# Layer 0's feed-forward for latent and context tokens in one set of gate and up products, with w2 accumulated in PSUM

## The chip, the cores and the metric

One core of a Trainium2 chip runs the whole program. The metric is the device time of one execution in microseconds, the median over runs. TensorE (PE) does the matmuls, VectorE (DVE), ScalarE (ACT) and GpSimd (POOL) the elementwise work, SyncE (SP) issues the DMAs; PE writes its sums to PSUM, eight banks of 512 float32 columns on 128 partitions, everything else lies in SBUF.

## The reference

Two transformer layers over 512 latent tokens and 256 context tokens of width 1024. What the change touches is layer 0's feed-forward (hidden width 2816), which both token kinds pass with the same weights and different modulation:

```python
def swiglu(h, w13, w2):
    gate, up = jnp.split(h @ w13, 2, axis=-1)
    return (jax.nn.silu(gate) * up) @ w2
...
x = x + mx[:, 2] * rmsnorm(yx, norm_g[l, 1])
hx = modulate(rmsnorm(x, norm_g[l, 2]), mx[:, 3], mx[:, 4])
x = x + mx[:, 5] * rmsnorm(swiglu(hx, ffn_w13[l], ffn_w2[l]), norm_g[l, 3])
if ctx_out:
    ctx = ctx + mc[2] * rmsnorm(yc, norm_g[l, 1])
    hc = modulate(rmsnorm(ctx, norm_g[l, 2]), mc[3], mc[4])
    ctx = ctx + mc[5] * rmsnorm(swiglu(hc, ffn_w13[l], ffn_w2[l]), norm_g[l, 3])
```

Layer 1 (latent attention) takes keys and values from both streams, and only the latent stream is returned. Its own feed-forward has latent tokens alone.

## The kernel before

**Products.** Every float32 operand is split into a high part (ACT casts it to float32r) and a low part (DVE subtracts: `sub`, line 127). A product is three matmuls, high by high, high by low and low by high. So each weight block that PE needs costs one ACT cast and one DVE subtraction (`block`).

**Seven products for eight.** Gate and up of the latent tokens run on 2x2 blocks (input halves by token halves of 256 columns) with seven block products in place of eight. The activations' seven combinations are made once, into `T` (`wino_first`, `wino_rest`); the weights' combinations s1 to s4 are made for every matrix.

**Layer 0.** `out_proj` takes the six token blocks in the order 0 to 5 (4 and 5 are context), and for the latent ones norms the result and fills `T`. Then `Ffn.x_pass` runs over eleven pairs of hidden blocks: gate and up for 512 latent tokens (`product`, line 1185), and for every two pairs `down_group` (line 1109): w2 with seven products for eight, whose sums DVE adds to `yx` in SBUF (line 1117). In `x_pass` s1 and s2 go to GpSimd from the third pair on (to DVE before), s3 and s4 always go there, and so do the sums of `down_group` (lines 1124 and 1127). The context tokens' norm stands inside the first pair (`ctx_norm`) and goes through DRAM. Then `c_pass` loads and splits all gate and up weights again for the 256 context columns, with plain products (tile `cg`, line 230), and w2 again in sevens. Between its pairs stand layer 1's latent keys (`kv_lat`) and query products (`qps`, line 1560).

**Layer 1.** `FfnWide` (lines 1327 and 1420) runs gate and up for the 512 latent tokens in sevens with s1, s2, s4 on DVE into PSUM and s3 on GpSimd, keeps all hidden activations in SBUF, and then adds up the plain w2 products in eight PSUM banks. Eight buffers for split weight blocks.

**Order.** One scheduler orders all instructions of an engine at build time from its own estimate; an engine works in that order and waits on semaphores. SP's queue is such an order too: a DMA that waits for a buffer holds those behind it. All weights pass three staging buffers (`wst`).

## Time and profile before

| | us |
|---|---|
| runs (three) | 1804.38, 1811.73, 1814.94 |
| median | 1811.73 |
| profiled execution, its time | 1804.81 |
| its span | 1803.0 |
| out-projection's end of layer 0 to layer 1's first scores | 680.0 |
| PE busy over the span | 1690.3 |
| mean granted clock | 0.982 |

The profiled execution is one of the program; its span is what the engines' rows cover. Busy shares are averages over stages with different limits, so the stretches are read apart. A matmul's listed length holds its latency; how many start in a stretch tells its pace.

### The profile page before, as it was taken

Reading aid. Unit: us, or ns where it says so; the run is one execution under the profiler, and the core shown is the slowest. Engines: PE = TensorE matmul, PEld = TensorE weight load, DVE = VectorE, ACT = ScalarE, POOL = GpSimd, SP = SyncE. Lnnn points to the kernel's source line nnn. Section 1 sums busy time; section 2 is a strip of 40 time slices with the busy share of each in tenths; the row PEclk is TensorE's granted clock in tenths of the full one; section 3 lists DMA queues with packets and bytes.
Section 4 is the critical chain, followed back from the end, with each engine's and each line's share of the span. In section 5 each row is a group of like instructions: output and inputs, shape, how many; then the busy total and the mean of one; then the engine's idle time right before and its main releaser. Section 6 shows DMA issues by size and latency. Waiting matters only on the chain. (4 is left out here: it accounts for less than half of the span.)

```text
span 1803.0 us, 29499 instructions
## 1 busy us (share of the span) xinstructions
PE 1690.3 (94%) x10860; PEld 1465.6 (81%) x10860; DVE 1362.0 (76%) x2048; ACT 963.5 (53%) x2012; POOL 709.9 (39%) x610
## 2 busy tenths in 40 slices
PE   7999999999888998999989899899999989999998
PEld 3588886568787887888978799789967889999886
DVE  3436888565899999899899988788867678877333
ACT  4325666564665454444665445667656655555332
POOL 2202344542476858757364542232222333322001
PEclk9999999999999999999999999999999999999999
DMA  9531226873343222232646443233363523333332
GB/s 366 170 94 34 61 51 187 241 232 127 126 144 117 71 94 87 78 117 64 211 158 195 147 152 115 71 81 71 91 179 98 170 85 118 95 114 98 115 96 82
DMA packets 67744, 225.48 MB, mean 125 GB/s; under 512 B 8208, under 2 KB 11408, under 8 KB 67600
## 3 DMA queue, kind: packets, MB, share of 16 engines
q1 hardware_dynamic: 67600, 223.61, 39.4%
q8 instruction: 85, 1.39, 0.3%
q14 instruction: 59, 0.48, 0.1%
HBM read 196.31 MB, written 10.49 MB: 115 GB/s over the span
## 5 line engine op out<-in xcount | busy, mean ns | idle before, releaser
L127 DVE TENSOR_TENSOR wl<-wst,wh 128x512 fp32r<-128x512 f32 (+2 forms) x329 | 313.5, 967 | 109.8 <-ACT wh L1319 69.3
L130 POOL TENSOR_SCALAR p<-p,sum 128x768 f32<-128x768 f32 (+2 forms) x96 | 82.5, 860 | 270.7 <-DVE sum L627 237.3
L127 DVE TENSOR_TENSOR wl<-S,wh 128x512 fp32r<-128x512 f32 x148 | 159.3, 1088 | 16.6 <-ACT wh L1053 8.9
L230 PE MATMUL cg<-h,wh 128*128 128x256 f32 x704 | 137.6, 293 | 2.6 <-ACT wh L1053 2.6
L1185 PE MATMUL A<-T,wh 128*128 128x256 f32 x704 | 135.6, 287 | 4.6 <-DVE g L1238 2.8
L230 PEld LDWEIGHTS cg<-h,wh 128*128 128x128 f32 x704 | 116.5, 200 | 6.0 <-ACT wh L1053 2.8
L1185 PEld LDWEIGHTS A<-T,wh 128*128 128x128 f32 x704 | 113.7, 194 | 9.1 <-DVE g L1238 3.6
L1327 PE MATMUL A<-T,wh 128*128 128x256 f32 x640 | 116.5, 283 | 2.1 <-ACT wh L1319 1.3
L230 PE MATMUL cg<-h,wl 128*128 128x256 f32 x352 | 103.6, 296 | 15.6 <-DVE wl L127 15.6
L1053 ACT CAST wh<-wst 128x512 fp32r<-128x512 f32 (+1 forms) x162 | 96.5, 611 | 38.2 <-PE cg L230 25.9
L1319 ACT CAST wh<-wst 128x512 fp32r<-128x512 f32 x104 | 63.7, 619 | 86.5 <-PE y L1420 68.5
L1185 PE MATMUL A<-T,wl 128*128 128x256 f32 x352 | 100.0, 286 | 5.4 <-DVE wl L127 5.3
L127 DVE TENSOR_TENSOR ptl<-tp,pth 128x512 fp32r<-128x512 f32 x124 | 84.2, 686 | 24.9 <-ACT pth L638 24.3
L230 PE MATMUL fps<-hT,wh 128*128 128x512 f32 (+1 forms) x416 | 96.3, 350 | 6.0 <-DVE KS L127 3.9
L1327 PEld LDWEIGHTS A<-T,wh 128*128 128x128 f32 x640 | 99.1, 192 | 2.5 <-ACT wh L1319 1.5
L638 ACT CAST pth<-tp 128x512 fp32r<-128x512 f32 x124 | 71.7, 587 | 47.8 <-PE tp L635 42.7
L1109 PE MATMUL y<-w2l,ah 128*128 128x512 f32 x210 | 85.2, 406 | 5.3 <-DVE w2l L127 5.2
L1327 PE MATMUL A<-T,wl 128*128 128x256 f32 x320 | 89.1, 284 | 1.0 <-DVE wl L127 1.0
L1109 PE MATMUL y<-w2h,al 128*128 128x512 f32 x210 | 82.6, 402 | 6.5 <-DVE al L127 6.5
L1053 ACT CAST wh<-S 128x512 fp32r<-128x512 f32 x88 | 53.4, 619 | 62.4 <-POOL S L1204 37.2
L230 PEld LDWEIGHTS cg<-h,wl 128*128 128x128 f32 x352 | 69.6, 198 | 20.2 <-DVE wl L127 19.2
L230 PEld LDWEIGHTS fps<-hT,wh 128*128 128x128 f32 x416 | 63.6, 189 | 25.9 <-issue 5.9
(451 smaller groups left out, 5366.4 us busy)
## 6 DMA issues: line engine op xcount, KB each, us to landing
wst<-in_wpk SPq DMA_DIRECT2D x147, 512.0 KB, 3.9
wst<-in_ada_w SPq DMA_DIRECT2D x80, 512.0 KB, 4.7
wst<-in_ffn_w SPq DMA_DIRECT2D x26, 512.0 KB, 3.5
w<-in_ffn_w SPq DMA_DIRECT2D x20, 512.0 KB, 4.4
S<-in_ffn_w SPq DMA_DIRECT2D x20, 512.0 KB, 4.5
wst<-in_ada_w SPq DMA_DIRECT2D x32, 256.0 KB, 6.6
xd<-xt SPq DMA_DIRECT2D x10, 512.0 KB, 2.6
xt<-in_x SPq DMA_DIRECT2D x8, 512.0 KB, 4.4
```

The costliest lines, as they stand in the source:

```text
L127: nc.vector.tensor_sub(out, a, hi.bitcast(F32))
L130: nc.gpsimd.tensor_scalar(out, a, s, 1.0, op0=ALU.mult, op1=ALU.mult)
L230: nc.tensor.matmul(ps, s, mov(k)[m], start=(k == 0 and i == 0), stop=(k == n - 1 and i == 2))
L638: nc.scalar.copy(h, tp[:, 0:P * n])
L1053: nc.scalar.copy(h, src)
L1109: nc.tensor.matmul(ps[t], a[x][:, f, P * t:P * t + P], b[y][:, f, :], start=(start and f == 0 and i == 0), stop=(f == 1 and i == 2), skip_ ...
L1185: nc.tensor.matmul(ps, x, T[m][:, i, k, :], start=(start and k == 0 and j == 0), stop=(stop and k == 3 and j == 2), skip_group_check=True)
L1319: nc.scalar.copy(h, src)
L1327: nc.tensor.matmul(ps, x, self.T[m][:, i, k, :], start=(start and k == 0 and j == 0), stop=(stop and k == 3 and j == 2), skip_group_check= ...
```

## The change

Layer 0's feed-forward goes over to `FfnWide`, with 384 columns a half: blocks 0, 1 (latent) and 4 (context) are the first half, 2, 3 and 5 the second. `out_proj` takes the token blocks in the order 0, 1, 4, 2, 3, 5, norms context blocks as well, and writes the first four combinations of `T`; the last three are written by `rest()` after it, in a second pool that opens when `out_proj`'s pools are closed. `x_pass`, `c_pass` and `down_group` go. `hidden` makes all gate and up activations once (eleven pairs). Then w2 is run twice with plain products, each time with its own load and split of the weights: for the latent tokens into eight PSUM banks, and for the context tokens, which GpSimd has copied aside (`keep_ctx`), into four. Four buffers for split weight blocks stand where layer 1 has eight, and two `down` steps are held back to the end where layer 1 holds four. The norm that opens layer 1 is taken out of the first w2 pass and put between steps of the second (`norm_x0`, which loads the latent rows back from DRAM), with `kv_lat`. The query products follow the second pass.

```diff
-    T = out_proj(0, QO, d["ab_w_out"], x_in, lambda t: xd[0][t], attention_end, (0, 1, 2, 3, 4, 5), s_o)
+    T, rest = out_proj(0, QO, d["ab_w_out"], x_in, lambda t: xd[0][t], attention_end, (0, 1, 4, 2, 3, 5), s_o)
     s_o.close()
+    T.add(pool(s_t, "T0b", side="right"), 4, 3, 384)
+    rest()
...
+        def rest():
+            for i, (a, b) in enumerate(zip(FIRST_HALF, SECOND_HALF)):
+                wino_rest(src, T, P * a, P * b, P * i, ts, (1,))
+        return T, rest
...
-    ff.x_pass(T, lambda t: xd[0][t], finish_x0, cpool, ctx_norm, ctx_load)
...
+    fw = FfnWide(0, T, 384)
+    fw.open(s_w, "fw0", 4)
...
+    fw.hidden(s_h, pool(s_g, "fg0"), between={6: gates})
...
+    def keep_ctx(k):
+        if k % 2 == 0:
+            nc.gpsimd.tensor_copy(gc[:, k:k + 2, :].rearrange("p i (h c) -> p i h c", h=2),
+                                  fw.g[k // 2].rearrange("p i (h c) -> p i h c", h=2)[:, :, :, 256:384])
...
+    def residual_x0(t):
+        xt = row("xt", 2)
+        nc.sync.dma_start(xt, xd[0][t])
+        residual(ys[t], xt, gg_x, row("tmp"))
+        nc.sync.dma_start(xd[1][t], xt)
+
+    fw.down(lambda k: half_cols(k, 0, 256), ys, residual_x0, 2, keep_ctx)
...
+    def norm_x0(t):
+        xt = row("xt", 2)
+        nc.sync.dma_start(xt, xd[1][t])
+        norm_mod(xt, row("tmp"), 1, 0, 0, psf, "B", half, into(hx3, P * t))
...
-    yc = fc.c_pass(hc, kv_lat_x)
...
+    def between_c(k):
+
+        if k % 3 == 1 and k < 12:
+            norm_x0(k // 3)
+        if k == 6:
+            kv_weights()
+        if k in (9, 12, 15, 18):
+            kv_lat(k // 3 - 3, scratch, "k")
...
+    fw.down(lambda k: gc[:, k, :], yc, residual_c0, 2, between_c)
```

PE's order where layer 0's feed-forward begins, first before, then now. `y` is the output projection, `ggt` a gate row and `ntp` the transposes of a token block's normed rows; `A` and `B` are the first two gate products.

```order
L293 MATMUL ggt<-ident,ggc_103 128x128 x8
L230 MATMUL y<-wl,oh 128x512 x2
L230 MATMUL y<-wh,ol 128x512 x2
L230 MATMUL y<-wh,oh 128x512 x2
L230 MATMUL y<-wl,oh 128x512 x2
L230 MATMUL y<-wh,ol 128x512 x2
L1185 MATMUL A<-T_4374,wh 128x256
```

The same place of PE now, where the gate products have line 1092:

```order
L230 MATMUL y<-wh,oh 128x512
L230 MATMUL y<-wl,oh 128x512 x2
L230 MATMUL y<-wh,ol 128x512 x2
L323 MATMUL ntp<-ident,xn 128x128 x16
L1092 MATMUL A<-T_4374,wh 128x384
L1092 MATMUL A<-T_4375,wh 128x384
```

Two blocks' transposes, those of token blocks 3 and 5, now stand between the last output-projection matmul and the first gate product.

DVE's order at the same place, before: the last residual steps, then the sums and low parts of the first weight blocks.

```order
L349 SCALAR_TENSOR_TENSOR xn<-y,rer,xn 128x512 x2
L350 TENSOR_TENSOR xt<-xt,xn 128x512
L1202 TENSOR_TENSOR S<-wst 128x512
L127 TENSOR_TENSOR wl<-wst,wh 128x512
L1203 TENSOR_TENSOR S<-S,wst 128x512
L127 TENSOR_TENSOR wl<-wst,wh 128x512 x2
```

Now, in two pieces: from the scale-and-shift behind the last block's transposes (line 332) on, and the end of the run that follows. `T_4375` holds the low parts of the first four combinations, `T_5002` those of the last three; `hf` is a difference of blocks. Eleven rows of `T_5002` and `hf` alone lie between the pieces.

```order
L319 TENSOR_SCALAR xn<-xt,nor 128x512
L127 TENSOR_TENSOR T_5002<-hf,T_5001 128x4x128
L332 TENSOR_SCALAR QO<-ntp,amod_100,mod_97 128x128 x4
L1103 TENSOR_TENSOR S<-wst 128x512
L127 TENSOR_TENSOR T_4375<-QO,T_4374 128x4x128
L1104 TENSOR_TENSOR S<-S,wst 128x512
L127 TENSOR_TENSOR T_4375<-hf,T_4374 128x4x128
L1105 TENSOR_TENSOR S<-wst,S 128x512
```

And DVE's end of that run, up to the first low weight parts:

```order
L127 TENSOR_TENSOR T_5002<-hf,T_5001 128x4x128 x2
L945 TENSOR_TENSOR hf<-QO,hf 128x512
L127 TENSOR_TENSOR T_5002<-hf,T_5001 128x4x128
L127 TENSOR_TENSOR wl<-wst,wh 128x512 x3
L127 TENSOR_TENSOR wl<-S,wh 128x512
```

The first low weight part (`wl`), which PE's third matmul of `A` needs, stands behind all of `T`.

SP's queue around the last write of layer 0's latent result (`xd1_3_116`), before and now, with buffer numbers: `wst` are the staging buffers, `in_ffn_w2` w2, `in_wpk` the packed weights.

```order
L1479 DMA xd1_3_116<-S_9207 128x1024
L1072 DMA S_9833<-in_ffn_w2 128x1024 x2
L204 DMA wst_9944<-in_wpk 128x1024
L204 DMA wst_10102<-in_wpk 128x1024
L1072 DMA S_9981<-in_ffn_w2 128x1024 x2
L204 DMA wst_10137<-in_wpk 128x1024
```

SP's queue from the same write on, now:

```order
L1263 DMA xd1_3_116<-xt_9090 128x1024
L1292 DMA xt_9188<-xd1_0_113 128x1024
L1292 DMA xt_9301<-xd1_1_114 128x1024
L204 DMA wst_9336<-in_ffn_w2 128x1024
L1292 DMA xt_9426<-xd1_2_115 128x1024
L204 DMA wst_9362<-in_ffn_w2 128x1024
L204 DMA wst_9388<-in_wpk 128x864
L1292 DMA xt_9581<-xd1_3_116 128x1024
L204 DMA wst_9392<-in_wpk 128x864
L1352 DMA xt_10018<-xd0_4_111 128x1024
L204 DMA wst_9396<-in_wpk 128x576
L204 DMA wst_9400<-in_ffn_w2 128x1024
```

The reloads of the latent rows (`xt`, two buffers) now stand between the loads of w2; before, w2 and packed weights followed each other.

## Rows read from the trace of the kernel before

**Rows 1.** The page, part 1: busy time (us), share of the span and number of instructions of every engine over the whole span.

```profile
PE 1690.3 (94%) x10860; PEld 1465.6 (81%) x10860; DVE 1362.0 (76%) x2048; ACT 963.5 (53%) x2012; POOL 709.9 (39%) x610
```

**Rows 2.** Busy time by stretch (us from the span's start : end, length, then busy us and number of instructions of PE, PE's weight loads, DVE, ACT and POOL; last the granted clock, the DMA share and GB/s). First row: from the end of layer 0's output projection to the first attention scores of layer 1. Second: the part of it in which `x_pass` runs. Third: `c_pass`. Fourth: gate and up products of layer 1's feed-forward (`FfnWide.hidden`).

```profile
481.60:1161.60 680.00, 610.78 (x4021) 560.00 (x4020) 617.21 (x745) 360.04 (x724) 387.46 (x253) 0.96 0.38 124
483.40:870.00 386.60, 346.75 (x2301) 317.85 (x2302) 359.83 (x388) 191.11 (x369) 257.47 (x160) 0.96 0.32 104
870.00:1112.70 242.70, 221.42 (x1479) 204.13 (x1478) 220.43 (x288) 139.55 (x279) 114.51 (x69) 0.96 0.52 169
1468.00:1675.50 207.50, 203.95 (x1691) 202.93 (x1691) 166.45 (x281) 116.12 (x250) 61.85 (x49) 1.00 0.34 108
```

**Rows 3.** What one matmul takes in a stream without gaps. The first two rows are stretches of layer 1's feed-forward, in the columns of rows 2: one of 256-column matmuls only (gate and up), one of 512-column matmuls only (w2). The last two are from PE's timeline (start us, length us, line, operation, output, inputs, form, number): the first and the 32nd of layer 1's query products, 384 columns; 31 start from the one to the other.

```profile
1500.00:1650.00 150.00, 150.00 (x1253) 150.00 (x1253) 118.75 (x203) 83.70 (x182) 47.27 (x37) 1.00 0.34 105
1680.00:1790.00 110.00, 110.00 (x487) 91.09 (x486) 39.41 (x60) 33.33 (x64) 4.31 (x6) 1.00 0.25 82
...
1114.21 0.33 PE L1560 MATMUL qps<-wh,hx 128*128 128x384 f32 x1
...
1119.61 0.51 PE L1560 MATMUL qps<-wh,hx 128*128 128x384 f32 x2
```

**Rows 4.** Matmul counts of layer 0's feed-forward. The first row is the stretch of rows 2's first row with the instructions of line 1185 alone (gate and up products of the latent tokens); the second with those that touch a tile named `y` (w2 products of both token kinds); their columns are PE, weight loads, and for `y` also DVE and ACT. The last two are groups of the page (line, engine, operation, output<-inputs, form, count | busy us, mean ns | idle us before, and what ended it): gate and up products of the context tokens.

```profile
481.60:1161.60 680.00, 250.27 (x1848) 242.06 (x1848) 0.96 0.38 124
481.60:1161.60 680.00, 192.63 (x703) 127.22 (x702) 71.58 (x108) 8.24 (x16) 0.96 0.38 124
...
L230 PE MATMUL cg<-h,wh 128*128 128x256 f32 x704 | 137.6, 293 | 2.6 <-ACT wh L1053 2.6
...
L230 PE MATMUL cg<-h,wl 128*128 128x256 f32 x352 | 103.6, 296 | 15.6 <-DVE wl L127 15.6
```

**Rows 5.** VectorE groups between 483 and 870 us (`x_pass`), columns as in the groups of rows 4: the subtractions that make the low part of a weight block, from a block `S` that was added up before and from a block as loaded.

```profile
L127 DVE TENSOR_TENSOR wl<-S,wh 128x512 fp32r<-128x512 f32 x88 | 118.6, 1362 | 8.9 <-ACT wh L1053 8.9
L127 DVE TENSOR_TENSOR wl<-wst,wh 128x512 fp32r<-128x512 f32 x66 | 83.5, 1285 | 1.4 <-ACT wh L1053 1.4
```

**Rows 6.** The same for layer 1's feed-forward, 1468 to 1800 us, whose sums `S` lie in PSUM (104 blocks as loaded: 60 in gate and up, 44 in w2); then a sum of blocks, and one step that takes a product out of PSUM; last, from the same stretch of ACT, the cast that makes the high part.

```profile
L127 DVE TENSOR_TENSOR wl<-wst,wh 128x512 fp32r<-128x512 f32 x104 | 79.8, 777 | 69.9 <-ACT wh L1319 69.3
L127 DVE TENSOR_TENSOR wl<-S,wh 128x512 fp32r<-128x512 f32 x60 | 40.8, 686 | 7.7 <-ACT wh L1319 6.9 <-PE A L1327 0.5
...
L1338 DVE TENSOR_TENSOR S<-wst 128x512 f32<-128x512 f32 x20 | 14.0, 700 | 22.0 <-DMA wst<-in_wpk 21.9
...
L1394 DVE TENSOR_TENSOR E<-A,E 128x256 f32<-128x256 f32 x10 | 4.2, 420 | 1.3 <-PE A L1327 1.3
...
L1319 ACT CAST wh<-S 128x512 fp32r<-128x512 f32 x60 | 35.1, 588 | 36.6 <-PE C L1327 16.9 <-PE A L1327 14.1 <-DVE S L1340 3.7
```

**Rows 7.** GpSimd groups of layer 1's feed-forward, same stretch: the one sum of blocks a matrix that is left to it, and the gate-times-up product of 256 columns.

```profile
L1341 POOL TENSOR_TENSOR s<-wst 128x512 f32<-128x512 f32 x19 | 33.3, 1754 | 97.4 <-DMA wst<-in_wpk 73.4 <-issue 12.8 <-DVE wl L127 6.8
L1395 POOL TENSOR_TENSOR g<-g,E 128x256 f32<-128x256 f32 x30 | 28.8, 961 | 53.5 <-DVE E L1394 44.6 <-ACT wh L1319 8.9
```

**Rows 8.** Who waited for whom on PE, 483 to 870 us and 870 to 1162 us (us in total, times, longest us): the largest entry of each.

```profile
PE B L1185 <- DVE wl L127: 14.4, 4, 3.6
...
PE cg L230 <- DVE wl L127: 15.6, 13, 2.9
```

**Rows 9.** PE's timeline where layer 0's feed-forward begins (idle us before and its releaser in brackets): the last output-projection matmuls, the first gate product, and the matmul after the longest wait. Then busy time, columns as in rows 2, of the five us before and after that one's start.

```profile
481.17 0.63 PE L230 MATMUL y<-wh,ol 128*128 128x512 f32 x2
483.42 0.50 PE L1185 MATMUL A<-T,wh 128*128 128x256 f32 x2 [1.63 <-ACT wh L1053]
...
489.16 0.58 PE L1185 MATMUL A<-T,wl 128*128 128x256 f32 x1 [4.72 <-DVE wl L127]
...
485.00:490.00 5.00, 0.84 (x4) 0.84 (x5) 4.96 (x6) 0.87 (x2) 3.14 (x3) 0.71 0.57 207
490.00:495.00 5.00, 5.00 (x29) 5.00 (x29) 5.00 (x8) 3.88 (x10) 1.45 (x1) 0.61 0.78 266
```

**Rows 10.** The end of layer 1's output projection, five timeline rows of four engines: the first square of the last token block's result (ACT), the transposes of that block's normed rows (PE), the first scale-and-shift behind them (DVE), GpSimd's differences of blocks, and the last low parts of T (DVE).

```profile
1438.79 0.58 ACT L310 ACTIVATE junk<-y 128x512 bf16<-128x512 f32 x1
...
1451.13 1.04 PE L323 MATMUL ntp<-ident,xn 128*128 128x128 f32 x8
...
1451.93 1.36 DVE L332 TENSOR_SCALAR OT<-ntp,amod,mod 128x128 f32<-128x128 f32 x4
...
1453.44 2.96 POOL L927 TENSOR_TENSOR hf<-OT 128x512 f32<-128x512 f32 x2 [5.86 <-DVE OT L332]
...
1459.57 1.42 DVE L127 TENSOR_TENSOR T<-hf,T 128x512 fp32r<-128x512 f32 x2
```

**Rows 11.** VectorE groups between 870 and 1162 us, columns as in rows 5: low parts of weight blocks and of the 256-column activations.

```profile
L127 DVE TENSOR_TENSOR wl<-wst,wh 128x512 fp32r<-128x512 f32 x90 | 85.3, 965 | 5.5 <-ACT wh L1053 3.7 <-ACT wh L211 1.5
...
L127 DVE TENSOR_TENSOR al<-g,ah 128x256 fp32r<-128x256 f32 x32 | 18.2, 568 | 0.0
```

**Rows 12.** DMA issues (kB each, median us from issue to landing): the w2 rows that go through the three staging buffers, as `FfnWide` loads them.

```profile
wst<-in_ffn_w SPq DMA_DIRECT2D x26, 512.0 KB, 3.5
```

**Rows 13.** Where a line's instructions start: min, median and max ns, first and last start (us). Layer 1's query products, and the first of the three groups of layer 1's w2 matmuls; then, from PE's timeline, layer 1's first attention scores.

```profile
L1560 PE MATMUL qps<-wh,hx x64: 333/334/346, 1114.2 to 1131.1; 128*128 128x384 f32 x64
...
L1420 PE MATMUL y<-wh,ah x176: 389/389/396, 1675.5 to 1794.6; 128*128 128x512 f32 x176
...
1161.59 1.23 PE L1693 MATMUL scm<-K,Q 96*128 96x512 f32 x3
```

More of the change, by code (lines that the diff above doesn't have):

```diff
@@ L919, in wino_rest @@
[L919 to L933 removed]
+        T = Blocks()
@@ new lines, in attention_end, with __init__, add, span @@
+        tpool = pool(s_t, "T0a", side="right")
+        T.add(tpool, 0, 4, 384)
+        return T, tpool
+    FIRST_HALF, SECOND_HALF = (0, 1, 4), (2, 3, 5)
+    class Blocks:
+        def __init__(self):
+            self.parts = []
+        def add(self, pl, first, n, cols):
+            t = [pl.tile([P, n, 4, cols], F32R, tag=f"T{m}", name=f"T{m}") for m in range(2)]
+            self.parts.insert(0, (first, first + n, t))
+        def span(self, m, i, n=1):
+            a, _, t = next(p for p in self.parts if p[0] <= i < p[1])
+            return t[m][:, i - a:i - a + n]
+        def at(self, m, i, k):
+            return self.span(m, i)[:, 0, k, :]
+        def put(self, i, n, c, src):
+            o = self.span(0, i, n)[:, :, :, c]
+            nc.scalar.copy(o, src)
+            sub(self.span(1, i, n)[:, :, :, c], src, o)
@@ new lines, in build, with half_cols @@
+    fw.hidden(s_h, pool(s_g, "fg0"), between={6: gates})
+    s_h.close()
+    s_t.close()
+    s_t = ExitStack()
+    rows = pool(s_t, "rows0", side="right")
+    cx = pool(s_t, "cx", side="right")
+    gc = cx.tile([P, NF, NC], F32, tag="cx", name="gc")
+    s_y, s_f = ExitStack(), ExitStack()
+    fw.open_acts(s_y, "fa0", 2)
+    psy = psum(s_y, "ps_y0")
+    ys = [[psy.tile([P, 512], F32, tag=f"y{t}{j}", name="y") for j in range(2)] for t in range(4)]
+    def half_cols(k, a, b):
+        return fw.g[k // 2][:, k % 2, :].rearrange("p (h c) -> p h c", h=2)[:, :, a:b]
@@ new lines, in build, with residual_c0 @@
+    yc = [[psf.tile([P, 512], F32, tag="c", name="yc") for _ in range(2)] for _ in range(2)]
+    gg_c = []
+    xc = []
+    def residual_c0(t):
+        if not gg_c:
+            gg_c.append(gate_row(1))
+        xc.append(row("xt", 2))
+        nc.sync.dma_start(xc[t], xd[0][4 + t])
+        residual(yc[t], xc[t], gg_c[0], row("tmp"))
+    fw.down(lambda k: gc[:, k, :], yc, residual_c0, 2, between_c)
+    k = krT[:, 0:NX]
+    rope(k, k, tabm[0:32], 8, scratch()[0:32])
+    key_rope(slice(0, NX))
@@ new lines, in build @@
+    pss = [psf.tile([P, 512], F32, tag=tag, name="qps") for tag in "kkBB"]
+    for k in range(NK):
+        if k % 2 == 0:
+            st = packed(f"mq{k // 2}")
+        w = fw.block(st[:, 384 * (k % 2):384 * (k % 2) + 384])
+        for t in range(4):
+            for n, (a, b) in enumerate(((0, 0), (0, 1), (1, 0))):
+                nc.tensor.matmul(pss[t][:, 0:384], hx3[a][:, k, P * t:P * t + P], w[b],
+                                 start=(k == 0 and n == 0), stop=(k == NK - 1 and n == 2))
@@ L1570, in build @@
+    s_w.close()
+    hc3 = cx.tile([P, 2, NK, NC], F32R, tag="cx", name="hc3")
+    hc3 = [hc3[:, m] for m in range(2)]
+    for t in range(2):
+        norm_mod(xc[t], row("tmp"), 1, 0, 1, psf, "c", half, into(hc3, P * t))
+    for t in range(4):
+        lat_T(t, pss[t], col("qg"), qT, 3, 0, scratch, "c")
     s_l1 = ExitStack()
```

508 lines of the change are left out of this document (120 added, 388 removed).

## The prediction

> **What bounds the kernel now.** I read first the stage windows, then what each matmul takes when nothing holds it up, then who waits. PE is busy for 94% of the span [rows 1], but that hides two kinds of stage. From the end of layer 0's output projection to layer 1's first scores, 680.0 us, PE is busy 610.8 us and its clock stood at 0.96 on average, while DVE is busy 617.2 us; in `x_pass` DVE is busy 359.8 of 386.6 us [rows 2]. In layer 1's gate and up products, the same arithmetic in the other form, PE is busy 204 of 207.5 us at full clock and DVE 166 [rows 2].
>
> The pace of a gapless stream says what the 680 us ought to hold. 1251 matmuls of 256 columns in 150 us (1253 touch the window, two of them cut) are 0.120 us each, 485 of 512 columns in 110 us 0.2267 us, and 31 of 384 columns from 1114.21 to 1119.61 us 0.1742 us [rows 3]: columns at 2.4 GHz, plus 13 to 14 ns. Layer 0's feed-forward has 1848 + 1056 matmuls of 256 columns and 702 of 512 [rows 4]: 348.5 + 159.1 = 507.6 us. Keys, queries and transposes there are an estimate of 51 us at the same paces. So about 120 of the 680 us are waits and half clock. The waits end on DVE's low weight parts in both passes [rows 8]. There one takes 1.29 us from a block as loaded and 1.36 us from a sum of blocks [rows 5]; in layer 1 they take 0.78 and 0.69 us [rows 6]. The difference beside them is GpSimd, busy 257 of 387 us in `x_pass` and 62 of 207 in layer 1 [rows 2], and sums that lie in SBUF there and in PSUM here.
>
> **The change part by part.**
>
> *PE's own work hardly shrinks.* Gate and up: 1848 matmuls of 384 columns, 1848 x 0.1742 = 321.9 us, in place of 2904 x 0.120 = 348.5. w2: plain products, 22 steps x (4 + 2 token blocks) x 6 = 792 x 0.2267 = 179.5 us in place of 159.1. Together 6 us less. What the change can win is the 120 us.
>
> The Trainium skill ("TensorE: Matmul & The Clock Gate", section "Wait — 56ns, not 53.3ns?") gives a warm matmul columns / 2.4 GHz + 2.5 ns. By it the two terms would be 300 and 171 us, 30 us less than by rows 3. Three widths here agree on 13 to 14 ns, so the measurement decides, and the page's value gets no chance of its own.
>
> *Start, 31 us (16 to 37).* Before, the context blocks came last and needed no transposes, so T was ready when `y` ended at 481.6 us, and the stall was 1.6 and 4.7 us, to 489.2 [rows 9]. Now the transposes of block 5 stand on PE ahead of the first gate product. The nearest chain is layer 1's: from the first square of the last block to its transposes 1451.1 - 1438.8 = 12.3 us [rows 10]. Behind them DVE has, before the first low weight part, one scale-and-shift of four (1.36 us, rows 10) and 18 other operations at 0.7 us, some 14 us; in layer 1 the half of that list took from 1451.9 to 1461.0 [rows 10], and its `hf` buffers, two, tie it to GpSimd's 1.5 us differences [rows 10]. I add 3 us for these. PE meets four matmuls and then waits: 12.3 + 14 + 3 = 29 us, plus 2 us, since after the last such stall the clock stood at 0.61 on average for five us, between its levels of 1.2 and 2.4 GHz [rows 9]. The low end is DVE doing the older blocks' part of T before the transposes (16 us), the high end each GpSimd difference exposed. Nothing hides this: all four engines serve the one chain.
>
> *Gate and up, 329 us (324 to 345).* DVE per pair: 6 low parts at 0.78, 8 from sums at 0.69 to 0.78, 6 sums at 0.70, and 7 steps out of PSUM at 0.42 for 256 columns [rows 6], at most 0.63 for 384: 4.7 + 5.8 + 4.2 + 4.4 = 19.1 us. PE needs 168 x 0.1742 = 29.3 us a pair, so DVE is no longer the bound; in layer 1 it was 166 against 204 and PE still ran at full clock. Layer 1 took 207.5 us for 1680 matmuls worth 201.6 [rows 2, 3]; I add the same 6 us and 1 for the second gate row: 321.9 + 7 = 329. Four weight buffers stand for eight: a block is free when its product ends, three products (6.3 us) before PE comes round, against 0.59 us of cast and 0.69 of subtraction [rows 6]; I cost it at nothing, and it is a rival below.
>
> *w2 for the latent tokens, 120 us (118 to 124).* The same 528 matmuls as layer 1's, first start 1675.5, last 1795 [rows 13]. 5.4 us a step against two loads' worth of slack; a load lands in 3.5 us [rows 12].
>
> *w2 for the context tokens with layer 1's norm and keys, 92 us (82 to 112).* PE: 264 x 0.2267 = 59.8, keys 96 x 0.133 (288 columns, between the paces of rows 3) = 12.8, 44 transposes at 0.13 [rows 10] = 5.7, in all 78.3 us. DVE per step 2 x 0.97 + 0.57 = 2.5 us [rows 11] against PE's 2.72 us, and norms and keys besides: the two run level. Entering, the banks of the latent sums must be emptied by `residual`: 2 us, since the second block's banks come first. Then SP's queue: loads from the sixth step on stand behind the reload of the latent rows, and each reload behind a free row buffer, so behind the norm of an earlier block on ACT, GpSimd and DVE. A load needs 3.5 us to land [rows 12] plus the split. I count 12 us of PE waits (4 to 30) over steps 6 to 9, until the queue holds only weights again.
>
> *Query products to the first scores, 47.4 us (44 to 53).* Unchanged in kind: 1114.2 to 1161.6 us now [rows 13]. The context residual and norm are hidden by the 16.7 us of query products as before.
>
> *Sum.* 31 + 329 + 120 + 92 + 47 = 619 us in place of 680.0, a gain of 61 us. The execution that the trace shows took 1804.8 us, so 1744 us; the median of the three runs lies 7 us above it, which would give 1751. I say **1747 us**. Terms at their ends together with the choice of base give 1728 to 1772 for this forecast.
>
> **Rivals.**
>
> *Quick start and loads in time.* If block 5's chain overlaps T's older parts (16 us) and the loads arrive ahead (4 us of waits), 15 + 8 us less: **1724**. For it: ACT was busy only 0.9 of five us there [rows 9]. Against: the order puts the low weight parts behind all of T.
>
> *DVE stays the bound.* At `x_pass`'s durations DVE would need 6 x 1.29 + 8 x 1.36 + 6 x 0.70 + 4.4 = 27 us a pair [rows 5, 6], close to PE's 29.3, and the context pass is level anyway. In `x_pass` the stretch took 1.2 times its PE work of 323 us; at half of that surplus gate and up cost 32 us more: **1779**. For it: GpSimd still has products of 384 columns and copies. Against: GpSimd's sum falls to 2 x 1.75 + 3 x 1.44 = 7.8 us a pair [rows 7]. The Trainium skill ("SBUF — State Buffer", section "Who interferes with whom") says that a DVE instruction with two SBUF inputs waits for a GpSimd one that reads SBUF, and one with a PSUM input doesn't. The rows agree (1.36 against 0.69 us); by it even all of GpSimd's time on top leaves DVE under PE.
>
> *Slower: four buffers are too few.* If the cast and subtraction (0.59 + 0.69 us) stood open before every other of the 154 block products, 77 x 1.3 = 100 us: **1847**. It decides from 0.4 us a product on, where the gain of 61 us is used up. Against: no such wait in layer 1, though with eight buffers.
>
> *It does not do what it says.* If PE's own work is the limit throughout, as 94% suggests, only the 6 us are won: **1806** on the median.
>
> **How the numbers follow.** Forecast 67%, quick start 14%, DVE still bound 10%, too few buffers 5%, PE's work alone 4%. All but the last two are faster by over 0.5% (about 9 us, what a measurement of this kernel can tell): 0.91; within 0.5%: 0.04; slower: 0.05. For 8 in 10 the range takes the forecast's 1728 to 1772, most of the quick start and half of the bound DVE: 1722 to 1785.
>
> **What would show it.** PE idle some 25 us between the last output-projection matmul and a steady stream of 384-column gate products, ended by DVE's low weight parts; then eleven pairs in about 30 us each at full clock, low parts under 0.8 us; 120 us of w2 without a gap; in the context pass waits on the casts of freshly loaded weights around steps 6 to 9. Wrong would be low parts above 1.2 us in the gate and up products, PE waits before most products there, a context pass above 112 us, or a matmul of 384 columns above 0.18 us.

## The result, and the profile after

The changed kernel takes 1766.28 us (median of 4 runs, 1764.67 to 1767.71) against 1811.6 us (4 runs, 1804.38 to 1814.94): ratio 0.9755, 95% interval 0.9724 to 0.9786. The profiled execution took 1765.6 us with a span of 1763.8 us; before, 1804.8 and 1803.0.

The page's first part after, in the columns of [rows 1]:

```profile
PE 1656.6 (94%) x9894; PEld 1442.0 (82%) x9894; DVE 1094.9 (62%) x1881; ACT 887.0 (50%) x1878; POOL 455.1 (26%) x488
```

TensorE's share has not moved; VectorE fell from 1362 to 1095 us and GpSimd from 710 to 455. Next the stretch from the end of layer 0's output projection on, in the columns of [rows 2]: to the first gate product; gate and up; w2 for the latent tokens; w2 for the context tokens with norm and keys; query products to the first scores of layer 1; and from there to the first products of the next head's keys (`knps`).

```profile
481.60:520.70 39.10, 4.48 (x19) 3.25 (x17) 28.18 (x39) 17.73 (x39) 19.68 (x18) 0.56 0.07 27
520.70:847.60 326.90, 324.61 (x1864) 323.27 (x1864) 185.34 (x299) 145.46 (x274) 79.99 (x62) 1.00 0.24 80
847.60:967.50 119.90, 119.86 (x528) 99.13 (x529) 45.26 (x72) 40.68 (x80) 6.80 (x9) 1.00 0.32 108
967.50:1064.80 97.30, 83.27 (x405) 69.13 (x404) 63.32 (x118) 56.12 (x136) 16.05 (x25) 0.93 0.56 189
1064.80:1114.40 49.60, 37.33 (x209) 34.11 (x208) 33.87 (x63) 25.74 (x69) 13.62 (x24) 0.90 0.21 53
1114.40:1130.40 16.00, 14.62 (x90) 13.45 (x90) 8.06 (x17) 8.30 (x19) 2.26 (x3) 0.90 0.35 93
```

The first five rows are 632.8 us, where 680.0 stood [rows 2]. The last must be read with them, because PE's order changed: before, the first value and query products (`vps`, `qnps`, from 1156.0 us on) stood ahead of the first scores, and now they follow the first of them. So these 16.0 us were 8.4 (first scores 1161.6, first `knps` 1170.0 us). Up to that point the gain is 47.2 - 7.6 = 39.6 us, and the span's gain is 39.2: the rest of the program takes the same time as before.

From the first gate product to the last context product PE idled 61 us before (39.9 + 21.3, [rows 2]) and idles 16 us now. Its busy time there fell from 568 to 528 us, though the work at full pace shrank by about 6: the rest is time that products took longer before, at a mean clock of 0.96. Gate and up now run at full clock with hardly a gap, and the low weight parts have lost their surcharge (VectorE groups from 530 to 840 us, columns as in [rows 5]; `s` is the sum that GpSimd leaves in SBUF):

```profile
L127 DVE TENSOR_TENSOR wl<-wst,wh 128x512 fp32r<-128x512 f32 x64 | 45.2, 706 | 27.0 <-ACT wh L1084 27.0
L127 DVE TENSOR_TENSOR wl<-S,wh 128x512 fp32r<-128x512 f32 x64 | 43.7, 684 | 8.4 <-ACT wh L1084 8.3
L127 DVE TENSOR_TENSOR wl<-s,wh 128x512 fp32r<-128x512 f32 x22 | 15.2, 693 | 28.8 <-ACT wh L1084 28.8
```

0.71 and 0.68 us stand where 1.29 and 1.36 stood [rows 5].

What the forecast and the trace say, term by term:

| stretch | forecast, us | after, us |
|---|---|---|
| start, to a steady stream | 31 | 40 |
| gate and up | 329 | 326 |
| w2, latent tokens | 120 | 119.9 |
| w2, context tokens, norm, keys | 92 | 97.3 |
| query products to first scores | 47.4 | 49.6 |
| from there to the next head's keys | 8.4 (not named) | 16.0 |

(The start is 39 us to the first gate product and about 1 us of slow products behind it; the clock averaged 0.70 in the five us from there.) Three places lost 24 us against the forecast (9 at the start, 5 in the context pass, 10 around the first scores); gate and up came out 3 us better.

**The start.** PE's waits from 481 to 523 us (us in total, times, longest us), then the last block's transposes on PE and rows of ScalarE's timeline (idle before and its releaser in brackets):

```profile
PE A L1092 <- ACT wh L1084: 20.3, 1, 20.3
PE ntp L323 <- ACT xn L318: 14.3, 2, 7.4
```

```profile
498.44 1.97 PE L323 MATMUL ntp<-ident,xn 128*128 128x128 f32 x8 [6.90 <-ACT xn L318]
...
505.94 0.62 ACT L929 CAST T<-hf 128x512 fp32r<-128x512 f32 x1 [2.47 <-POOL hf L945]
...
517.43 0.62 ACT L929 CAST T<-hf 128x512 fp32r<-128x512 f32 x1 [0.50 <-POOL hf L945]
519.53 0.62 ACT L929 CAST T<-hf 128x512 fp32r<-128x512 f32 x1 [1.49 <-DVE hf L945]
520.06 1.66 ACT L1084 CAST wh<-wst 128x512 fp32r<-128x512 f32 x3
```

From 505 us on each cast of a block of T waits in turn for a difference `hf` from VectorE or GpSimd, for 0.5 to 2.5 us, and the first weight casts (`wh`) stand behind the last of them. The first gate products need only blocks among T0 to T3, whose last cast ended near 503 us. Against the forecast's terms: the last transposes began 16.8 us behind the output projection (forecast 12.3), and the first gate product 22.3 us behind them (forecast 14 + 3).

**The context pass.** PE's waits from 960 to 1070 us, then rows of VectorE, of ScalarE and of SP's queue there:

```profile
PE yc L1186 <- DVE wl L127: 5.9, 1, 5.9
PE yc L1186 <- ACT ah L1176: 4.9, 1, 4.9
...
PE yc L1186 <- DVE tmp L349: 1.6, 1, 1.6
```

```profile
976.24 0.69 DVE L350 TENSOR_TENSOR xt<-xt,tmp 128x512 f32<-128x512 f32 x1 [3.25 <-DMA xt<-xd]
...
980.65 0.68 DVE L127 TENSOR_TENSOR wl<-wst,wh 128x512 fp32r<-128x512 f32 x1
```

```profile
986.35 0.63 ACT L310 ACTIVATE junk<-xt 128x512 bf16<-128x512 f32 x1 [13.27 <-DMA xt<-xd]
...
989.90 0.39 ACT L1176 CAST ah<-gc 128x256 fp32r<-128x256 f32 x1
```

```profile
981.21 4.14 SPq L1292 DMA_DIRECT2D xt<-xd  x2
985.41 0.42 SPq L204 DMA_DIRECT2D wst<-in_ffn_w  x1
```

The three long waits end at 969.9, 981.4 and 990.3 us, at the entrance of the pass and not around steps 6 to 9. The low part behind the 5.9 us (980.65) stood on VectorE behind the residuals of the last latent blocks, one of which had waited 3.3 us for its row, loaded into one of two buffers. At 981 us SP's queue spends 4.1 us on the norm's reloads of latent rows, with a weight load behind them; on ScalarE the norm's first square came after 13.3 idle us, ended by that row's landing, and the cast of the next activations (`ah`, 989.90), which ended the 4.9 us, stood behind it.

**Behind the query products.** From the end of the query products to the first `knps`, before and after, in the columns of [rows 2]:

```profile
1131.40:1170.00 38.60, 32.00 (x194) 27.30 (x192) 28.62 (x60) 23.68 (x60) 8.13 (x14) 0.96 0.30 74
```

```profile
1081.50:1130.40 48.90, 35.25 (x203) 30.92 (x201) 29.71 (x62) 24.61 (x62) 7.67 (x15) 0.86 0.25 61
```

PE idles 13.7 us where it idled 6.6. Its busy time is 3.3 us longer, at a mean clock of 0.86 instead of 0.96, and the products are not quite the same: nine more stand in this stretch, six of layer 1's first key products (`early<-kvT,hx`, ahead of the query products before, at 1112.7 us, and behind them now, at 1096.6) and three transposes of context rows. At the full pace of [rows 3, 10] the nine are some 1.8 us (an estimate). PE's longest waits there after:

```profile
PE ltp L1304 <- DVE ln L1299: 5.8, 2, 3.5
PE ntp L323 <- ACT tmp L318: 2.2, 1, 2.2
PE ltp L1304 <- DVE nh L1299: 2.1, 1, 2.1
```

### The profile page after: what moved, and what is told of

The parts are those of the page before. It is cut to its first block, busy times and chain, and to the rows that moved or that the text cites. A ratio compares the mean times of both kernels' runs of the same rounds, so it can differ in the third digit from the quotient of the medians.

```text
span 1763.8 us, 26987 instructions
## 1 busy us (share of the span) xinstructions
PE 1656.6 (94%) x9894; PEld 1442.0 (82%) x9894; DVE 1094.9 (62%) x1881; ACT 887.0 (50%) x1878; POOL 455.1 (26%) x488
## 5 line engine op out<-in xcount | busy, mean ns | idle before, releaser
L1092 PE MATMUL A<-T,wh 128*128 128x384 f32 (+1 forms) x1344 | 293.0, 311 | 22.0 <-ACT wh L1084 20.5
L1092 PE MATMUL A<-T,wl 128*128 128x384 f32 (+1 forms) x672 | 204.8, 311 | 1.0 <-DVE wl L127 1.0
L1092 PE MATMUL C<-T,wh 128*128 128x384 f32 (+1 forms) x672 | 149.1, 310 | 1.0 <-ACT E L1110 0.6
L1186 PE MATMUL y<-wh,ah 128*128 128x512 f32 x352 | 136.4, 389 | 1.0 <-ACT ah L1176 1.0
L1186 PE MATMUL y<-wl,ah 128*128 128x512 f32 x352 | 136.8, 389 | 0.0
L1186 PE MATMUL y<-wh,al 128*128 128x512 f32 x352 | 135.6, 389 | 0.0
L1092 PEld LDWEIGHTS A<-T,wl 128*128 128x128 f32 x672 | 127.1, 190 | 1.4 <-DVE wl L127 1.3
L1092 PEld LDWEIGHTS C<-T,wh 128*128 128x128 f32 x672 | 113.2, 190 | 1.5 <-ACT E L1110 0.9
L1092 PE MATMUL C<-T,wl 128*128 128x384 f32 (+1 forms) x336 | 104.1, 310 | 0.0
L1499 PE MATMUL scm<-K,Q 96*128 96x512 f32 (+1 forms) x384 | 83.6, 349 | 2.3 <-ACT p L621 1.3
```

Of the source, the lines that this page charges most:

```text
L1092: nc.tensor.matmul(ps, x, self.T.at(m, i, k), start=(start and k == 0 and j == 0), stop=(stop and k == 3 and j == 2), skip_group_check=True)
L1186: nc.tensor.matmul(ys[t][j], a[x][:, P * t:P * t + P], w[j][y], start=(k == 0 and i == 0), stop=(k == NF - 1 and i == 2))
L1499: nc.tensor.matmul(ps[:, k0:k1], Q[0:96, e, a, P * i:P * i + P], K[0:96, e, b, k0:k1], start=(n == 0), stop=(n == 2))
```

## The experiments

Times are medians; the kernel after is 1766.3 us. It was timed with the first result only; the kernel before, timed again beside each group of runs, had medians from 1807.2 to 1811.6 us. So a difference of less than some 4 us between two medians of different groups says little by itself, and stretches of the traces are compared with those of the kernel after. Theory and rival are those of the expectation in front of each result.

**The first gate products ahead of the last blocks of T.** `matrix` is cut so that its first three products can be issued earlier; the weight buffers move to the other end of SBUF and are opened anew for w2. `ahead` splits four weight blocks and issues three products:

```diff
+    fw = FfnWide(0, T, 384)
+    fw.open(s_w, "fw0", 4, side="right")
+    fw.ahead(s_h)
     rest()
```

> The kernel after, but the weight blocks of the first three gate products are split, and these products issued, before the last three blocks of T (T4 to T6, nine casts) are made. Theory 'program order': in the kernel after, the first gate product has T0 to T3 from about 503 us on and waits until 520.7 only because the cast of its weights stands on ScalarE behind all T casts. Then PE does 36 matmuls (6.3 us) inside that wait: the first gate matmul starts near 506 us, and the time falls by 6 to 7 us, to about 1760 us. Rival 'one chain': VectorE and ScalarE are the limit of the start, and the splits put ahead (4 to 5 casts of 0.6 us, as many low parts of 0.7 us) push T4 to T6 back by as much: the fifth product starts at the same time or later, and the time stays at 1764 to 1768 us.

1763.9 us (1761.7 to 1767.6). PE's waits from 482 to 870 us, those of the transposes left out:

```profile
PE A L1093 <- ACT T L929: 3.3, 1, 3.3
PE y L1207 <- ACT ah L1197: 2.6, 1, 2.6
PE A L1093 <- ACT wh L1085: 2.5, 1, 2.5
```

The 20.3 us wait is gone and the first gate product starts at 500.8 us, but PE then waits for T itself and for splits between T's casts. The first w2 product comes 3.7 us sooner after the projection than in the kernel after, with 1.6 us more of wait at the reopened buffers. Both theories hold in part: the program's order cost something, and the splits do compete with T's blocks. The 2.4 us in the median are too few to show it; the trace's 3.7 us are what speaks for it.

**Three `hf` buffers.** The edit does two things: it adds the third buffer, and it counts `hf` apart from the rows `xn`, with which it shared a counter, so that two differences in a row could fall to the same buffer when a row came between them.

```diff
-            self.n += 1
-            i = self.n % 2
             if tag == "xn":
+                self.n += 1
+                i = self.n % 2
                 return self.x[:, 1024 * i:1024 * i + 1024]
+            self.m += 1
+            i = self.m % 3
```

> The kernel after with three instead of two buffers for the differences hf from which T's blocks are cast. Theory 'ring': from 502 to 520 us each cast waits for an hf buffer and each difference for a free one, so that ScalarE, VectorE and GpSimd take turns; a third buffer takes 3 to 5 us off the start (first gate matmul near 516 to 518 us) and the time falls to about 1762 us. Rival 'VectorE is full': it has 21 operations there and is busy 74% of 480 to 522 us; the first gate matmul moves by under 1 us and the time stays within 1765 to 1768 us.

1757.4 us (1757.0 to 1758.7), 8.9 us less. PE's waits from 480 to 870 us, then ScalarE's timeline:

```profile
PE A L1094 <- ACT wh L1086: 16.7, 1, 16.7
PE ntp L323 <- ACT xn L318: 10.9, 1, 10.9
```

```profile
504.53 1.89 ACT L929 CAST T<-hf 128x512 fp32r<-128x512 f32 x3 [1.88 <-POOL hf L945]
510.34 1.66 ACT L929 CAST T<-hf 128x512 fp32r<-128x512 f32 x3 [3.92 <-DVE hf L945]
511.91 1.66 ACT L1086 CAST wh<-wst 128x512 fp32r<-128x512 f32 x3
```

T's casts now come in groups of two and three without a wait between them, and the first gate product starts at 512.6 in place of 520.7 us. The theory was right and its price too low by half: the ring had held up the transposes of the last blocks as well (14.3 us of waits fell to 10.9; the last transposes begin at 493.95 in place of 498.44 us). What the buffer gave and what the counter gave was not tried apart.

**Latent rows kept.** Four row buffers in place of two; the norm takes the rows where they are.

```diff
-        xt = row("xt", 2)
-        nc.sync.dma_start(xt, xd[1][t])
-        norm_mod(xt, row("tmp"), 1, 0, 0, psf, "B", half, into(hx3, P * t))
+        norm_mod(xs[t], row("tmp"), 1, 0, 0, psf, "B", half, into(hx3, P * t))
```

(The gate row moves to the activations' pool to make room.)

> The kernel after, but the four latent rows keep four buffers of their own: they are all loaded ahead of the residuals, and the norm between the context steps takes them where they are in place of loading them back. Theory 'reloads on SP's queue': the three waits at the entrance of the context pass (1.6, 5.9 and 4.9 us, with half clock behind them) come from loads of rows that stand in front of weight loads, and of engines that stand behind a row that has not landed; without reloads the context pass takes 84 to 88 us in place of 97 and the time falls by 9 to 13 us, to 1753 to 1757 us. Rival 'the norm's own work': ScalarE, VectorE and GpSimd have the same residuals and norms to do; the waits shrink by under 4 us, and the time stays above 1762 us.

1760.3 us (1757.4 to 1761.0). The context pass took 85.9 us in place of 97.3, as the theory said; PE's waits from 845 to 1060 us:

```profile
PE y L1186 <- ACT ah L1176: 4.6, 1, 4.6
PE ntp L323 <- ACT tmp L318: 3.3, 1, 3.3
PE yc L1186 <- DVE tmp L349: 1.6, 1, 1.6
```

```profile
850.49 1.14 ACT L1176 CAST ah<-g 128x512 fp32r<-128x512 f32 x2 [3.48 <-POOL g L1161]
```

The time lies between theory and rival, because of the 11.4 us that the pass gave, 6.4 were lost before it: PE waited 4.6 us at the first w2 step for `ah`, which waited for GpSimd's last gate-times-up step (probably because the moved gate row shifts `ah` to the place of that step's operand), and the w2 products behind the wait took 2.7 us longer. The same wait of 4.6 us came in two later runs that moved the gate row.

**The work behind the query products in turn.**

```diff
+    K = whole(mla_keys(0, w1p, ps, [(ps, kv_x)]))
+    for t in range(4):
+        lat_T(t, pss[t], col("qg"), qT, 3, 0, scratch, "c")
+        if t < 2:
+            norm_mod(xc[t], row("tmp"), 1, 0, 1, psf, "c", half, into(hc3, P * t))
```

> The kernel after with the work behind the query products written in another order: layer 1's first keys of the latent tokens first, then the query latents in turn with the norm of the context rows, where the kernel after has both norms first, then the four query latents, then the keys. Theory 'order': behind the query products PE idles 12.3 us up to the first scores where the kernel before idled 6.5, because the work that could fill the gaps is queued behind the chain of query latents; with it in turn the idle time falls to 5 to 8 us and the time by 5 to 9 us, to 1757 to 1761 us. Rival 'the chain itself': the latents' chain of square, scale, transpose and split with its two buffers sets the end whatever stands between; the time stays at 1764 to 1768 us.

1764.5 us (1764.0 to 1765.5), as the rival said. From the first query product to `knps` it is 65.1 us (65.6 after), and the same waits remain:

```profile
PE ltp L1304 <- DVE ln L1299: 6.0, 2, 3.6
PE ltp L1304 <- DVE nh L1299: 2.6, 2, 2.4
```

**More scratch rows behind the query products.** (The gate row moved, as above.)

```diff
-        return lat.tile([P, 512], F32, tag="ln", name="ln", bufs=2)
+        return lat.tile([P, 512], F32, tag="ln", name="ln", bufs=4)
...
-        norm_mod(xc[t], row("tmp"), 1, 0, 1, psf, "c", half, into(hc3, P * t))
+        norm_mod(xc[t], row("tmp", 2), 1, 0, 1, psf, "c", half, into(hc3, P * t))
```

> The kernel after with four buffers in place of two for the latents' scratch rows (ln) and two in place of one for the norm's scratch row (tmp). Theory 'rings': with the written order ruled out by the run before, PE's 12 us of waits behind the query products come from small rings, since a query latent waits for the scratch rows of the one before and the second context norm for the first one's row; with more buffers the waits ended by ln and tmp (5.8 and 2.2 us) fall to under 3 us together, and the time falls by 4 to 7 us, to 1759 to 1762 us. Rival 'engine order': ScalarE, GpSimd and VectorE take the squares, scales and splits in a fixed order whatever is free, and the time stays at 1764 to 1768 us.

1762.9 us (1760.1 to 1765.3). The stretch behind the query products takes 63.0 in place of 65.6 us, less than the theory wanted; the context pass 91.8 in place of 97.3 (its norm uses `tmp` too); the first w2 step loses 3.8 and w2 2.6 us to the moved gate row, as in the run with rows kept.

**The sums of weight blocks in SBUF, and then by GpSimd.** These two undo a part of the change. They also leave one buffer in place of two for `s3`, the sum that GpSimd makes anyway, and move the gate rows' scratch to the new buffers. (`self.l` is the layer, 0 here.)

```diff
-            s1, s2, s4 = (self.ps.tile([P, 512], F32, tag="S", name="S") for _ in range(3))
-            s3 = self.ep.tile([P, 512], F32, tag="s3", name="s3", bufs=2)
+            s1, s2, s4 = ((self.ps if self.l else self.ep).tile([P, 512], F32, tag="S", name="S", **({} if self.l else {"bufs": 3})) for _ in range(3))
+            s3 = self.ep.tile([P, 512], F32, tag="s3", name="s3", bufs=1 + self.l)
```

In the second kernel `s2` and `s4` change like `s1`:

```diff
-            nc.vector.tensor_add(s1, a21, a22)
+            (nc.vector if self.l else nc.gpsimd).tensor_add(s1, a21, a22)
```

> The kernel after with layer 0's sums of weight blocks s1, s2 and s4 still made by VectorE, but written to SBUF (three buffers) in place of PSUM (four), with one buffer in place of two for the sum that GpSimd makes. Theory 'width': VectorE is no longer the bound because one split serves 384 columns; a low part from a sum gets dearer (0.69 us after, up to 1.36 where GpSimd runs beside it), VectorE goes from about 19 to 22 to 25 us a pair against PE's 29.3, and gate and up stay within 5 us of 326 us, the time at 1764 to 1772 us. Rival 'PSUM': taking the sums out of SBUF is what made the gain, and without it gate and up take over 20 us more, 1786 us or above.

> As the last, and the three sums made by GpSimd, as most of them were in the kernel before: GpSimd then has eight sums a pair (some 12 to 15 us) beside VectorE's splits. Theory 'width': low parts cost 1.2 to 1.4 us again, VectorE needs 4.4 + 14 x 1.3 = 22.6 us a pair, still under PE's 29.3: gate and up stay within 10 us of 326 us and the time under 1778 us. Rival 'placement': VectorE with GpSimd's contention is the bound again, gate and up take 345 us or more, and the time is 1786 us or above.

1770.4 us (1768.9 to 1771.9) and 1771.7 us (1770.6 to 1774.8). Gate and up of the second, with its low parts (530 to 840 us):

```profile
521.80:849.80 328.00, 324.92 (x1864) 323.61 (x1864) 165.54 (x236) 147.78 (x274) 160.82 (x125) 0.99 0.25 80
```

```profile
L127 DVE TENSOR_TENSOR wl<-S,wh 128x512 fp32r<-128x512 f32 x64 | 52.0, 813 | 38.7 <-ACT wh L1084 38.4
L127 DVE TENSOR_TENSOR wl<-wst,wh 128x512 fp32r<-128x512 f32 x63 | 47.9, 760 | 21.1 <-ACT wh L1084 21.1
L127 DVE TENSOR_TENSOR wl<-s,wh 128x512 fp32r<-128x512 f32 x21 | 21.2, 1009 | 22.2 <-ACT wh L1084 22.2
```

GpSimd is busy 161 of 328 us, twice as long as after, and low parts cost up to 1.01 us; still gate and up took 328.0 us against 326.9, the first kernel's 328.3 (the rest of their 4 to 5 us lies in the stages around). So the rivals are excluded: neither the place of the sums nor the engine that makes them was the gain; together with the `s3` buffer they are worth 1 to 2 us there. That leaves 'width': VectorE has room because one split now serves 384 columns and is made once for both kinds of tokens. This is argued from what is left and from VectorE's busy time (185 of 327 us after, 360 of 387 before in `x_pass`); no run took the width back by itself. Nor did one give VectorE back the sums of w2, 72 us in layer 0 before [rows 4]; spread over the eleven pairs they would bring it from 16.8 to some 23 us a pair, still under PE's 29.3 (an estimate from these rows). The Trainium skill ("SBUF — State Buffer", section "Who interferes with whom") has a VectorE instruction with two SBUF inputs contend with a GpSimd one that reads SBUF, and whichever starts second waits; the 1.01 us against the 0.69 us of the kernel after agree, but that it happens says nothing yet of the time, which hangs on whether VectorE is late.

**Three weight buffers.**

```diff
-    fw.open(s_w, "fw0", 4)
+    fw.open(s_w, "fw0", 3)
```

> The kernel after with three in place of four buffers for the weight blocks' two parts in layer 0's feed-forward. Theory 'four are just enough': one of them is held by the block whose product is put off, so three leave two that turn; a split (0.6 + 0.7 us) then has one product (2.1 us) of time when nothing else queues on ScalarE and VectorE, and some of the 154 products wait: 10 to 60 us slower, 1776 to 1826 us, with PE's waits ended by the low parts wl. Rival 'any ring will do': the split is short against a product and the time stays within 5 us.

1775.0 us (1773.3 to 1776.4), 8.7 us slower, between theory and rival. Gate and up:

```profile
520.20:851.30 331.10, 328.80 (x1865) 324.30 (x1865) 185.00 (x298) 145.35 (x273) 79.98 (x62) 0.99 0.25 80
```

PE is busy 328.8 us in place of 324.6 for the same products, and inside the stretch no wait is over 1.1 us: the cost is spread over many products. The rest of the 8.7 us are 1 to 2 us in each later stage. So four are close to the edge, at a small price, not at the 100 us of the prediction's rival.

**Key latents ahead of the early queries.**

```diff
+    for t in (4, 5):
+        kv_lat(t, lambda: rows.tile([P, 512], F32, tag="nh", name="nh", bufs=2), "k")
     RQ = whole(mla_rope(0, w1p, early()))
     KQ = [[K, whole(mla_queries(0, w1p, early(), RQ))]]
-    for t in (4, 5):
-        kv_lat(t, lambda: rows.tile([P, 512], F32, tag="nh", name="nh", bufs=2), "k")
```

> The kernel after with the two context blocks' key latents (kv_lat 4 and 5) written ahead of layer 1's first rotary and query products, where the kernel after has them behind. On PE the 11 matmuls that end the last key latent then stand ahead of 18 products of the early queries, not behind. Theory 'order at one place': the run that took the whole stretch in turn left this place as it was (its last key latent ended at 1107.3 us for one matmul that stood behind the 18); the end of the stretch hangs on this key latent, its split, the context keys and the first scores, so it ends about 4.2 us earlier, the time 3 to 5 us less: 1761 to 1763 us. Rival 'the queries end as late': the early queries, now behind, set the first scores by their own rotary and copies, and the time stays at 1765 to 1768 us.

1766.2 us (1765.4 to 1771.6), as the rival said. PE's timeline, then SP's queue:

```profile
1100.31 3.99 PE L230 MATMUL kvps<-hx,hc 128*128 128x288 f32 x24
1104.14 4.29 PE L230 MATMUL early<-qT,hx 128*128 128x512 f32 x18
...
1115.38 0.77 PE L1499 MATMUL scm<-K,Q 96*128 96x512 f32 x1 [2.29 <-issue]
```

```profile
1113.01 1.19 SPq L133 DMA_DIRECT2D Q<-RQ  x2
```

The last key latent ended 3.4 us sooner (1104.3 in place of 1107.7) and the early queries began 2.1 us later (1104.1, 1102.0); the copy of their rotary part (`Q<-RQ`) goes out at 1113.0 us and the first scores follow at 1115.4. The profile names no releaser there; in the run with four edits it puts 2.4 us of the first scores' wait down to that copy. So two chains seem to end together here, the key latent's and the queries'.

**Edits together.** First: three `hf` buffers; rows kept, but loaded at steps 8 to 11; two `tmp` rows in the activations' pool; key latents ahead of queries. (The gate row moved, as above.)

```diff
     def keep_ctx(k):
+        if 8 <= k < 12:
+            xs[k - 8] = row("xt", 4)
+            with tc.issue_after(latest(mybir.EngineType.SP)):
+                nc.sync.dma_start(xs[k - 8], xd[0][k - 8])
...
-        residual(ys[t], xt, gg_x, row("tmp"))
+        residual(ys[t], xt, gg_x, fw.ap.tile([P, D], F32, tag="tmp", name="tmp", bufs=2))
```

> The kernel after with four edits: three buffers for hf at the start; the latent rows kept in four buffers, loaded one at each of the steps 8 to 11 of the w2 products so that no load stands ahead of the first weights; two scratch rows for residual and norm; key latents ahead of the early queries. Theory 'the terms add': 8 to 9 us at the start, 10 to 13 us in the context pass (97.3 to 85 us, with nothing lost at the first w2 step this time), 3 to 5 us before the first scores, so 1766 less 21 to 27: 1739 to 1745 us. Rival 'one gives back the other': what is saved early turns into waits later, as the rows kept lost 3.6 us at the first w2 step, and the sum is under 17 us: 1749 us or above.

1751.6 us (1751.2 to 1754.0), 14.7 less, as the rival said. Start and context pass gave 8.1 and 11.5 us; the first w2 step took back 4.2 and w2 2.4, although no load of rows stood ahead of it, so that the pool's layout, not SP's queue, seems to make this wait. Then the first three gate products ahead as well, by the edit of the first experiment:

> The kernel of the run before (four edits) with the first three gate products and their splits ahead of the last blocks of T as well. Theory 'program order': with the ring of hf gone, PE still waits some 16 us for the first weights behind T's casts; 36 matmuls fit into it, gate and up end 4 to 6 us earlier, of which the reopened weight buffers take 2 at the first w2 step: 2 to 4 us less than the run before. Rival 'one chain': with three hf buffers VectorE and ScalarE have no gap left for the splits, T4 to T6 come later by as much, and the time is the same within 1.5 us or longer.

1747.6 us (1746.1 to 1748.5), 4.0 less, with a new wait at the entrance of the context pass (PE, 950 to 1047 us):

```profile
PE yc L1209 <- ACT ah L1199: 8.8, 1, 8.8
```

Last, the latent pass's activations at the other end of SBUF, and the rotary step of the latent keys at step 19 of the context pass:

```diff
-    fw.open_acts(s_y, "fa0", 2)
+    fw.open_acts(s_y, "fa0", 2, side="right")
...
+        if k == 19:
+            kr = krT[:, 0:NX]
+            rope(kr, kr, tabm[0:32], 8, scratch()[0:32])
+            key_rope(slice(0, NX))
```

> The kernel of the run before (five edits) with two more: the latent pass's activation and scratch buffers lie at the other end of SBUF, so that the context pass's first activations need not wait until the residual has left them; and the rotary step of the latent keys is taken during the context pass, where it stood beside the residual and norm of the context rows, behind the query products' start. Theory 'what was measured adds': in the run before PE waited 8.8 us at the first context step for casts that stood behind the residual on ScalarE; that wait falls to under 3 us, and the context rows' norm is ready 2 to 4 us earlier against the query products: 6 to 11 us less in all, 1737 to 1742 us. Rival 'work conserving': the residuals and norms of the latent rows need ScalarE, VectorE and GpSimd then anyway, and what is not waited at the first step is waited at the third or fourth: 1745 to 1749 us.

1744.0 us (1741.8 to 1747.9), between theory and rival: ratio to the kernel before 0.9647 (0.9624 to 0.9671), the fastest of all.

```profile
PE yc L1209 <- ACT ah L1199: 4.5, 1, 4.5
```

The entrance lost its wait (w2 of the latent tokens to the first context product 120.2 us in place of 130.6), and 5.3 of the 10.4 us came back inside the pass. The rotary step changed nothing: from the query products to `knps` 65.9 us.

## Why the prediction was right, and where it was off

The direction and its mechanism were right: PE's own work hardly shrank, and the gain came out of waits on low weight parts and the slow products beside them, gone from gate and up and from w2. Its size was off: 45 of the 65 us forecast, 1766.3 us against 1747 on the median, 1765.6 against 1744 for the profiled execution.

- **PE's pace and work**: right. 519 whole matmuls of 384 columns in the 90 us from 560 to 650 us are 0.173 us each (forecast 0.1742).
- **Start, 31 us**: 40, with two terms mis-sized: 16.8 in place of 12.3 us to the last transposes, 22.3 in place of 14 + 3 behind them. The step that failed is that the `hf` ring was priced at 3 us, for "its `hf` buffers, two, tie it to GpSimd's 1.5 us differences", and behind the transposes only; with a third buffer and a counter of its own the two parts took 12.4 and 18.6 us, 8 less. Also, PE waited for weight casts on ScalarE behind T's casts, not for VectorE's low parts: both engines have the first split behind all of T, so the quick start did not come. Taking splits ahead gave another 4 us on top of other edits.
- **Gate and up, 329 us, VectorE no longer the bound**: right, 326. The rival in which VectorE stays the bound is excluded: VectorE is busy 185 of 327 us. Even with the sums on GpSimd the stretch is 328.0 us, though low parts cost at most 1.01 us there and not the 1.3 of the rival.
- **Four weight buffers cost nothing**: not tried with more. One fewer costs 8.7 us, so the cover is thin; the rival's 100 us need far more than that.
- **w2 for the latent tokens, 120 us**: right.
- **Context pass, 92 us**: 97.3. The kind of cause was right, loads of latent rows and engines standing behind them. The place (steps 6 to 9) was wrong, and so was the split: the entrance, put at 2 us of `residual`, waited 7.5 us (1.6 + 5.9), the reloads, put at 12, some 6 (4.9 + 1.3). That the idle time came out as forecast (14 us; 97.3 - 83.3 = 14.0) is luck. PE's own work, put at 78.3 us, took 83.3 at a mean clock of 0.93: what follows a wait was not in the sum. With four row buffers and no reloads the pass took 85.9; what the buffers and what the missing reloads gave was not tried apart.
- **Query products to first scores, 47.4 us**: 49.6, and 7.6 more just behind. The step that failed is "Unchanged in kind". Six key products, 1.4 us at full pace, came into this stretch and stood in no term of the sum. And the context residual and norm are not hidden as before: after, the second context row is scaled 3.2 us behind the last query product (ScalarE's step ends at 1084.7, the products at 1081.5), where before it was 0.9 us ahead (1130.5 and 1131.4). Of the some 10 us, 7 are idle time of PE. Neither of two other orders nor an earlier rotary step changed the stretch; larger scratch rings gave 2.6. What makes the rest stays open. The last key latent, whose 24 products run from 1100 us on although its operands were ready near 1090, is not enough of a cause by itself: where it ended 3.4 us sooner, the first scores came no sooner.
- **Range, 1728 to 1772**: called the terms at their ends, but these add up to 584 and 671 us, which is 1709 to 1803 with either base. How it was narrowed is not said; 1766 lies near its upper end.

## What to carry to other kernels

When engines have slack in the bulk of a stage, look at its seams: they cost 24 us more than forecast here, while the two steady stages came out within 3 us. At a seam a two-deep ring crossed by three engines is a chain, to be costed at full length and not at the sum of one engine's work; and a buffer that is moved to make room can bring a wait into another stage (4.6 us at the first w2 step wherever the gate row was moved, except where the weight buffers moved too). A wait that an experiment removes should be followed to the end of the kernel: rows kept saved 11.4 us in their stage and 6 in the program.

## What was not expected of the hardware

Beside twice as much GpSimd work the mean low part from loaded blocks rose only to 0.76 us (0.71 after, 1.29 before), though both inputs lie in SBUF as before. The traces show why when the low parts are sorted by whether a GpSimd instruction was already running as they began. Where none was, they took 0.68 to 0.69 us in all three kernels. Where one was, they took 1.63 us on average in `x_pass` (42 of 66) and 0.92 with the sums on GpSimd (20 of 63): GpSimd was busy for 49% of that stretch against 67% of `x_pass`, and its instructions there took 1.3 us on average against 1.6. Low parts of sums in PSUM paid nothing: 18 of 64 began so in the kernel after, at 0.68 us.

And waits had a tail: after the 20.3 us wait the next five us ran at a mean granted clock of 0.70, between the levels of 1.2 and 2.4 GHz; behind the query products, with waits of 0.9 to 3.5 us, the clock averaged 0.86; and with the rows kept, the w2 products behind the 4.6 us wait started 0.43 us apart for some six us, where 0.23 is the full pace.
